# A woven RWKV scan: a later solve, DMA readers tied to program order, and loads issued from ScalarE's queue

## The chip, the cores and the metric

The kernel runs on one core of one Trainium2 chip. The metric is the device time of one execution in microseconds (us). The program is 52362 instructions long, without loops at run time: everything is unrolled when it is built.

## The reference, cut to what matters

Two layers of a diffusion backbone: 1024 latent tokens and 256 context tokens, 1024 channels. Each layer projects the modulated norm of the tokens into four head groups, mixes them, projects the result back with a gated residual, and ends with a SwiGLU FFN. The modulation vectors come from c and w_mod.

```
mod_x = (jax.nn.silu(c) @ w_mod[l] + b_mod[l])[:, None, :]
sh1, sc1, gt1, sh2, sc2, gt2 = jnp.split(mod_x, 6, axis=-1)
ux = _modulate(h, norm1_g[l], sh1, sc1) @ w_in[l]
...
h = h + gt1 * _mix_and_project(ux, y_rwkv_x, *other)
h = h + gt2 * _swiglu(_modulate(h, norm2_g[l], sh2, sc2), ffn_w_in[l], ffn_w_out[l])
```

The part that matters here is the RWKV-7 head group, a recurrence over tokens in both directions, four heads of 64 channels:

```
def step(S, inp):
    w_t, kk_t, a_t, k_t, v_t = inp[:5]
    sa = jnp.einsum('bhvk,bhk->bhv', S, -kk_t)
    S = (S * w_t[:, :, None, :] + sa[..., None] * (kk_t * a_t)[:, :, None, :]
         + v_t[..., None] * k_t[:, :, None, :])
    y = jnp.einsum('bhvk,bhk->bhv', S, inp[5]) if with_out else None
    return S, y
```

## The kernel before

The recurrence is cut into stages of 128 tokens for each direction, two chunks of 64 each: two stages for the context and eight for the latent tokens, ten in a layer. Inside a chunk the steps are replaced by matrix products, for which a triangular matrix has to be inverted for each head, direction and chunk.

A stage goes through these functions, all generators that hand control back at each `yield`:

- `prep` (L870 on) computes the decays and scaled keys of a stage.
- `inner` multiplies them (tiles ps), masks the products on VectorE (L982, four instructions a stage, tiles W), and stores the 32x32 diagonal blocks to a DRAM tile `Ad` (L986, eight DMAs). It loads all blocks back into two tiles `As`, each block row copied to four groups of 32 partitions (L992, two DMAs; in the rows this is `t<-Ad`, since all such tiles are called t). Then comes the solve: first the 4x4 diagonal blocks (L1020 to L1024, one half on VectorE, one on GpSimd after a memset, L1018), then eight block rows (L1032, L1033, L1039 to L1041) on VectorE, all with a raised priority (`s.ahead(SPRI)`). The last reduction, the eighth L1033, ends a solve. The inverse is stored to a DRAM tile `Td` (L1045) and loaded back in another layout into `TT` (L1051, four DMAs).
- `front_b` brings v into place, and merges the two 32x32 inverses into a 64x64 one: a transpose of TT on VectorE (L1091), two groups of small matmuls, and a copy by DMA (L1109).
- `chain` is the recurrence proper: per chunk the products G (copied by ScalarE at L1143), U (L1156), the new state (L1165) and y (L1178), each a group of small matmuls into a pc bank and a copy by ScalarE.
- `finish` adds the two directions, normalizes and gates; it reads what a stage in the other direction has stored.

`rwkv2` weaves them. In iteration `it` the chain of stage it runs beside `front_b` of stage it+1, `inner` of stage it+2 and `prep` of stage it+3, in 14 gaps (GAPS). Each gap advances every live generator by one `yield` (`W.step`), every second gap the chain by one step, and a budget of other matmuls is filled in (`W.fill`, FILL): dense projections, the Fourier mixer, the output projection `outp` and the context's FFN, all into pf banks. At the end of an iteration the generators that the next one needs are run out (`W.drain`). Buffers come from rings (`rg`): As has a depth of 1, Tt of 2, TT and W of 3.

Before that, `rwkv1` makes the projections while the convolution and the pooling run at their side. There the modulation of the first layer is also computed, in six pieces (j, half): by default `mod_sum`, on ScalarE and GpSimd for half 0 and on VectorE for half 1 (L257 and seven times L255 for each of two columns); pieces named in MODPE go to TensorE instead (`mod_pe`).

The order in which instructions stand on an engine is not the order in which they are written. A scheduler places them when the program is built, by priority (the order of writing, less what `ahead` subtracts) and by a model of when each becomes ready. On the chip each engine's queue then runs strictly in that order. All DMAs of this kernel are issued by SyncE (SP), whose queue is in order as well.

## Time and profile before

| | |
|---|---|
| median of 3 runs | 3368.19 us (3366.14 to 3374.23) |
| profiled execution | 3355.82 us, of which 3354.0 us are the span from first to last instruction |
| TensorE (PE) busy | 2962.7 us (88%) |
| VectorE (DVE) busy | 2136.8 us (64%) |
| ScalarE (ACT) busy | 1261.7 us (38%) |
| GpSimd (POOL) busy | 1395.4 us (42%) |
| mean granted TensorE clock | 0.912 of full speed |
| DMA | 415.48 MB, 39.5% of 16 engines, all on one queue |

Busy time is an average over stages with different limits, so it says little by itself. The views by stretch, the chain that ended last and the waits of each engine are read together: a stretch in which no engine is full has something in series, and the waits name it. A wait is printed as who waited, for whom, the total in us, how often, and the longest.

### The profile page before, as it was taken

How to read it: one execution, taken by the hardware profiler on the slowest of the kernel's cores; microseconds unless marked ns; L12 is line 12 of the kernel's file. 1: busy time of each engine (PE TensorE's matmuls, PEld its weight loads, DVE VectorE, ACT ScalarE, POOL GpSimd, SP SyncE). 2: the span in 40 equal slices, each digit the busy share in tenths (PEclk: the TensorE clock that was granted, in tenths of full speed). 3: DMA queues.
4: the chain of work that ended last, by engine and by line, in shares of the span. 5: the costliest groups of instructions: out<-in, count | busy, mean ns of one | idle time of the engine just before them, and what ended most of it. 6: DMA issues, size and time to landing. Idle time of an engine off the chain costs nothing.

```text
span 3354.0 us, 52362 instructions
## 1 busy us (share of the span) xinstructions
PE 2962.7 (88%) x18872; PEld 2391.2 (71%) x18872; DVE 2136.8 (64%) x3524; ACT 1261.7 (38%) x2575; POOL 1395.4 (42%) x1490
## 2 busy tenths in 40 slices
PE   6978898777989999999999978878776699999998
PEld 3757766665778888887888766645554478888887
DVE  6799766666566888644535597666575655555435
ACT  4555435344463322223212455333433433333312
POOL 2465324554268544444310154245541265454600
PEclk8979887788899999999999988878877799999999
DMA  7433345555464444336412222345553322224512
GB/s 265 148 99 105 102 117 143 148 152 156 142 215 153 143 134 151 112 106 225 141 29 90 75 69 95 106 130 142 163 143 83 129 76 82 88 76 134 171 40 77
DMA packets 375818, 415.48 MB, mean 124 GB/s; under 512 B 115587, under 2 KB 214916, under 8 KB 375558
## 3 DMA queue, kind: packets, MB, share of 16 engines
q1 hardware_dynamic: 375558, 412.13, 39.5%
q8 instruction: 149, 2.44, 0.3%
q14 instruction: 111, 0.91, 0.1%
HBM read 306.49 MB, written 100.27 MB: 121 GB/s over the span
## 4 chain that ended last, share of the span: by engine, by line
PE 58%; DVE 21%; DMA 11%; issue 4%; SPq 2%; ACT 2%; POOL 1%; DVEq 0%; POOLq 0%; ACTq 0%
PE pc L151 17%; PE ps L151 17%; PE pb L151 14%; PE pf L151 10%; DVE c L525 4%; DMA t<-Ad 3%; DMA Td<-t 2%; DVE t L1039 2%; DVE t L1032 1%; DVE t L255 1%; DVE t L947 1%; DVE g L1040 1%; DVE t L1041 1%; DVE f L319 1%; DMA Ad<-t 1%
## 5 line engine op out<-in xcount | busy, mean ns | idle before, releaser
L151 PE MATMUL pc<-t,f 128*128 128x512 f32 (+1 forms) x3108 | 744.8, 389 | 31.4 <-ACT t L420 18.7
L151 PEld LDWEIGHTS pc<-t,f 128*128 128x128 f32 x3108 | 575.3, 193 | 160.3 <-ACT t L420 22.9
L151 PE MATMUL ps<-t,f 128*128 128x512 f32 (+1 forms) x2094 | 517.7, 392 | 21.3 <-ACT t L318 7.6
L151 PE MATMUL pb<-t,f 128*128 128x512 f32 (+1 forms) x2094 | 467.5, 368 | 7.8 <-ACT t L1457 3.6
L151 PEld LDWEIGHTS ps<-t,f 128*128 128x128 f32 x2094 | 390.6, 190 | 102.2 <-ACT t L318 8.1
L151 PEld LDWEIGHTS pb<-t,f 128*128 128x128 f32 x2094 | 368.7, 189 | 77.7 <-ACT t L1457 4.4
L1504 ACT CAST f<-c 128x512 fp32r<-128x512 f32 x316 | 195.8, 621 | 529.3 <-PE ps L151 127.7
L1506 POOL TENSOR_TENSOR f<-c,f 128x512 fp32r<-128x512 f32 x135 | 185.8, 1377 | 429.3 <-ACT f L1504 424.2
L151 PE MATMUL pf<-t,f 128*128 128x512 f32 (+2 forms) x1500 | 311.1, 361 | 20.9 <-DMA f<-eo 10.0
L151 PEld LDWEIGHTS pf<-t,f 128*128 128x128 f32 (+1 forms) x1500 | 247.5, 197 | 66.5 <-issue 10.4
L318 ACT CAST f<-m 128x512 fp32r<-128x512 f32 (+1 forms) x236 | 135.5, 577 | 413.4 <-PE pb L151 218.6
L1506 DVE TENSOR_TENSOR f<-c,f 128x512 fp32r<-128x512 f32 x181 | 161.8, 894 | 139.5 <-ACT f L1504 134.5
L523 POOL TENSOR_TENSOR c<-c,cp 128x352 f32<-128x352 f32 (+2 forms) x168 | 185.4, 1104 | 151.5 <-ACT c L516 91.8
L151 PE MATMUL pf<-c,f 128*128 128x512 f32 (+1 forms) x704 | 212.0, 431 | 8.5 <-DVE t L1669 7.2
L319 POOL TENSOR_TENSOR t<-c,t 128x512 fp32r<-128x512 f32 (+1 forms) x110 | 138.1, 1294 | 163.0 <-PE ps L151 100.2
L151 PE MATMUL ps<-t,t 64*128 64x128 f32 (+2 forms) x1032 | 156.1, 342 | 54.9 <-DVE t L947 32.4
L151 PEld LDWEIGHTS ps<-t,t 64*128 64x128 f32 (+1 forms) x1032 | 129.9, 230 | 82.8 <-issue 26.3
L525 DVE SCALAR_TENSOR_TENSOR c<-c,dv,c 128x352 f32<-128x352 f32 (+2 forms) x238 | 186.9, 819 | 1.0
L255 DVE SCALAR_TENSOR_TENSOR cp<-m,sc,cp 128x512 f32<-128x512 f32 x140 | 138.5, 1010 | 51.9 <-DMA m<-in_wmod 51.1
L151 PE MATMUL pc<-t,t 128*64 128x64 f32 (+3 forms) x2484 | 137.8, 246 | 33.8 <-ACT t L1165 19.7
L151 PEld LDWEIGHTS pc<-t,t 128*64 128x64 f32 (+2 forms) x2484 | 111.9, 151 | 76.8 <-issue 24.4
L151 PEld LDWEIGHTS pf<-c,f 128*128 128x128 f32 x704 | 137.4, 222 | 39.8 <-DVE t L1669 7.8
(256 smaller groups left out, 4760.6 us busy)
## 6 DMA issues: line engine op xcount, KB each, us to landing
c<-in_ffin SPq DMA_DIRECT2D x176, 256.0 KB
m<-in_wmod SPq DMA_DIRECT2D x116, 256.0 KB
t<-rw SPq DMA_DIRECT2D x232, 128.0 KB
hid<-t SPq DMA_DIRECT2D x88, 256.0 KB
c<-hid SPq DMA_DIRECT2D x88, 256.0 KB
m<-in_ffout SPq DMA_DIRECT2D x80, 256.0 KB
t<-in_wmod SPq DMA_DIRECT2D x76, 256.0 KB
m<-in_win SPq DMA_DIRECT2D x64, 256.0 KB
```

The lines of the kernel that those rows point to most:

```text
L151: s.nc.tensor.matmul(o, l, r, start=start, stop=stop)
L255: nc.vector.scalar_tensor_tensor(acc[t], w, sc, acc[t], ALU.mult, ALU.add)
L318: s.nc.scalar.copy(hi, src)
L319: (eng or s.lo_eng).tensor_tensor(lo, src, hi.bitcast(F32), ALU.subtract)
L523: nc.gpsimd.tensor_tensor(g, g, t_, ALU.add)
L525: nc.vector.scalar_tensor_tensor(a, w[:, j:j + m], tap(j), a, ALU.mult, ALU.add)
L947: nc.vector.tensor_tensor(BKv[rows, :, :, 1 - h, :], cv(kd)[rows], cv(iP)[rows], ALU.mult)
L1032: nc.vector.tensor_tensor(tv, at(x, o, [0, m], [1, 4], [32, 4]), at(T_, r0, [32, m], [0, 4], [1, 4]), ALU.mult)
L1039: nc.vector.tensor_tensor(tv, at(x, o + 4, [0, m], [1, n], [32, 4]), at(T_, r0, [32, m], [0, n], [1, 4]), ALU.mult)
L1040: nc.vector.tensor_reduce(uv, tv, mybir.AxisListType.X, ALU.add)
L1504: nc.scalar.copy(hi, x)
L1506: (nc.gpsimd if s.nw % 7 in LOP else nc.vector).tensor_tensor(lo, x, hi.bitcast(F32), ALU.subtract)
```

## The change

The readers of data that come by DMA get `pin`: `keep_in_program_order` adds the rule that an instruction may not be placed ahead of what was written before it on its engine. The solve starts three steps later (SLAG), the merge three (MLAG), the read-out two (FLAG), the casts of `outp` four (OLAG). `inner` is run out in the middle of the next iteration rather than at the end of its own. Two more pieces of the modulation go to TensorE. The loads from Ad and from Td are issued by ScalarE, the first after the first half of the copies of T, the second two steps after the store.

```
-MLAG = 3
+MLAG = 6
+SLAG = 3
+FLAG = 4
...
-MODPE = ((3, 0),)
+MODPE = ((2, 1), (3, 0), (4, 1))
...
+    def pin(s, i):
+
+        return s.tc.keep_in_program_order(i)
...
     def split(s, src, hi, lo, eng=None):
-        s.nc.scalar.copy(hi, src)
+        r = s.nc.scalar.copy(hi, src)
         (eng or s.lo_eng).tensor_tensor(lo, src, hi.bitcast(F32), ALU.subtract)
+        return r
...
+                if g == GAPS // 2:
+                    W.drain(tx.get(it + 1))
...
-            for t in (tb_ if 0 <= it + 1 < N else None, tx.get(it + 2), tp if it + 3 < N else None):
+            for t in (tb_ if 0 <= it + 1 < N else None, tp if it + 3 < N else None):
                 W.drain(t)
...
-        for a in range(2):
-            nc.sync.dma_start(As[a], Adf[:, a * 512:(a + 1) * 512].unsqueeze(0).broadcast_to([4, 32, 512]))
...
             yield
+            if not d:
+                for a in range(2):
+                    s.pin(nc.scalar.dma_start(As[a], Adf[:, a * 512:(a + 1) * 512].unsqueeze(0).broadcast_to([4, 32, 512])))
+            yield
+        for _ in range(SLAG):
             yield
         s.lab(f"rsolve.{F.seg}{F.i}")
...
-            nc.gpsimd.memset(at(x, 16 * a, [33, 16]), 1.0)
+            s.pin(nc.gpsimd.memset(at(x, 16 * a, [33, 16]), 1.0))
             with s.ahead(SPRI):
-                e.tensor_tensor(t(0, [1, 2]), D(34, [33, 2]), D(1, [33, 2]), ALU.mult)
+                s.pin(e.tensor_tensor(t(0, [1, 2]), D(34, [33, 2]), D(1, [33, 2]), ALU.mult))
...
         nc.sync.dma_start(Td.rearrange("b u h (m par) i -> par (b u h) m i", par=4), Tt[:, 0:256])
+        for _ in range(2):
+            yield
+        s.lab(f"rsolve.{F.seg}{F.i}")
...
-                nc.sync.dma_start(TTv[r0:r0 + 32, :, 32 * b:32 * b + 32], Td[b, :, h].rearrange("u c i -> c u i"))
+                s.pin(nc.scalar.dma_start(TTv[r0:r0 + 32, :, 32 * b:32 * b + 32], Td[b, :, h].rearrange("u c i -> c u i")))
...
-            nc.scalar.copy(vr[:, p * 128:(p + 1) * 128], s.nat(F.v, p, 1))
+            s.pin(nc.scalar.copy(vr[:, p * 128:(p + 1) * 128], s.nat(F.v, p, 1)))
...
-        nc.vector.transpose(T1.rearrange("q (u i) -> q u i", i=32), TTv[:, :, 0:32])
+        s.pin(nc.vector.transpose(T1.rearrange("q (u i) -> q u i", i=32), TTv[:, :, 0:32]))
...
-        yield
-        yield
+        for _ in range(FLAG):
+            yield
         lab()
         for t_, w_ in ((y, w[0]), (ks, w[1])):
             hv = lambda a: a.rearrange("q (d n) -> q d n", d=2)
-            nc.vector.tensor_tensor(hv(t_), hv(t_), hv(w_)[:, ::-1, :], ALU.add)
+            s.pin(nc.vector.tensor_tensor(hv(t_), hv(t_), hv(w_)[:, ::-1, :], ALU.add))
...
-            s.split(y, *a)
+            late.append((y, a))
             acts.append(a)
+        for _ in range(OLAG):
+            yield None
+        for y, a in late:
+            s.pin(s.split(y, *a))
             yield 0.1
```

What the scheduler makes of it is shown for the last stage of layer 0, its matrices Ad (7682 before, 7554 in the change) and the inverse Td of the stage ahead of it (7649 before, 7660 in the change). Lines of the change are some 6 to 20 higher: L995 is the store to Ad, L1013 the load from it, L1057 the store to Td, L1066 the load from it, L991 the mask, L1032 the first step of a solve, L1045 its reduction, L1106 the transpose of TT, L1158, L1171, L1180 and L1193 the four copies of the chain, L1008 the copy of T.

SP's queue before:

```order
L1045 DMA Td_7649<-t_744_3437 4x256x32
L1337 DMA t_1461_8700<-ho_858 128x256
L1337 DMA t_1462_8701<-ho_859 128x256
L1337 DMA t_1462_8701<-ho_860 128x256
L1051 DMA t_958_4782<-Td_7649 32x8x32 x4
L986 DMA Ad_7682<-t_701_3210 32x4x32 x2
L986 DMA Ad_7682<-t_703_3212 32x4x32 x2
L1670 DMA ho_862<-t_1310_7621 128x512
L296 DMA m_1394_8249<-in_wout 128x512
L992 DMA t_721_3310<-Ad_7682 128x1x512
L992 DMA t_722_3311<-Ad_7682 128x1x512
```

SP's queue in the change:

```order
L995 DMA Ad_7554<-t_700_3187 32x4x32 x2
L995 DMA Ad_7554<-t_702_3189 32x4x32 x2
L876 DMA t_744_3427<-rw_897 128x2x128
L302 DMA m_1385_8205<-in_wout 128x512
L995 DMA Ad_7554<-t_701_3188 32x4x32 x2
L302 DMA m_1388_8211<-in_wout 128x256
L995 DMA Ad_7554<-t_703_3190 32x4x32 x2
L1680 DMA t_1450_8619<-hd_869 128x512
L1680 DMA t_1460_8667<-hd_870 128x512
L1057 DMA Td_7660<-t_751_3480 4x256x32
L302 DMA m_1400_8336<-in_wout 128x512
```

The stores to Ad, half of which stood behind the loads from Td, now stand ahead of the store to Td, and the two loads are gone from this queue.

ScalarE's queue in the change, where these loads went (before, no DMA stands in it):

```order
L1013 DMA t_721_3288<-Ad_7554 128x1x512
L1013 DMA t_722_3289<-Ad_7554 128x1x512
L1180 COPY t_880_4267<-pc_7672 64x2x128
L1180 COPY t_881_4268<-pc_7672 64x2x128
L1008 COPY t_723_3290<-ps_7686 128x256
L1008 COPY t_724_3291<-ps_7686 128x256
L1193 COPY t_957_4754<-pc_7725 128x2x64 x2
L1066 DMA t_983_4911<-Td_7660 32x8x32 x4
L353 ACT_TABLE_LOAD
L353 ACTIVATE t_811_3887<-pb_7753,cv 128x128
L324 CAST f_1374_8130<-m_1373_8128 128x256
L1158 COPY gg_7777<-pc_7768 128x256
```

The chain's copies of the new state (L1180) stand behind the loads from Ad, and its next copy of G (L1158) behind the loads from Td.

VectorE's queue before, from the end of one solve to the first step of the next:

```order
L1032 TENSOR_TENSOR t_744_3437<-t_722_3311,t_744_3437 128x128
L1033 TENSOR_REDUCE t_744_3437<-t_744_3437 128x8x4
L982 TENSOR_TENSOR t_701_3210<-ps_7708,cv 128x512
L982 TENSOR_TENSOR t_703_3212<-ps_7709,cv 128x512
L1669 SCALAR_TENSOR_TENSOR t_1310_7621<-pf_7623,mod_78,t_1310_7621 128x512
L1213 SCALAR_TENSOR_TENSOR t_886_4322<-pb_7772,t_886_4322 128x512
L1091 STREAM_TRANSPOSE t_853_4103<-t_958_4782 128x256
L347 RECIPROCAL t_813_3925<-t_813_3925 128x128
L1020 TENSOR_TENSOR g_7860<-t_721_3310 128x4x2
```

VectorE's queue in the change, from the last mask to the end of the solve ahead of the same one (the first step, L1032, stands three rows further down):

```order
L991 TENSOR_TENSOR t_703_3190<-ps_7607,cv 128x512
L1053 TENSOR_TENSOR t_751_3480<-t_751_3480,g_7325 128x6x8
L1044 TENSOR_TENSOR t_751_3480<-t_722_3289,t_751_3480 128x112
L1045 TENSOR_REDUCE t_751_3480<-t_751_3480 128x7x4
L1228 SCALAR_TENSOR_TENSOR t_884_4279<-pb_7720,t_884_4279 128x512
L1051 TENSOR_TENSOR t_751_3480<-t_722_3289,t_751_3480 128x112
L1052 TENSOR_REDUCE g_7325<-t_751_3480 128x28
L1053 TENSOR_TENSOR t_751_3480<-t_751_3480,g_7325 128x7x4
L1044 TENSOR_TENSOR t_751_3480<-t_722_3289,t_751_3480 128x128
L1045 TENSOR_REDUCE t_751_3480<-t_751_3480 128x8x4
L1688 SCALAR_TENSOR_TENSOR t_1317_7705<-pf_7707,mod_78,t_1317_7705 128x512
L354 RECIPROCAL t_811_3887<-t_811_3887 128x128
```

The last mask stood behind the end of the solve and now stands nine rows ahead of it. The transpose L1091, which stood ahead of the solve, is gone from here. In other stages of the change the masks still stand at the end of the solve.

## Rows read from the trace of the kernel before

**Rows 1.** Windows: stretch, length, busy us (instructions) of PE/PEld/DVE/ACT/POOL, granted clock, DMA share, GB/s.
```profile
504.60:865.00 360.40, 284.99 (x3020) 224.16 (x3019) 235.65 (x519) 156.10 (x409) 186.38 (x297) 0.81 0.54 150
2176.50:2585.00 408.50, 301.79 (x3174) 222.61 (x3174) 251.45 (x572) 155.25 (x413) 180.60 (x307) 0.78 0.48 133
168.00:252.00 84.00, 59.25 (x282) 45.25 (x282) 81.74 (x101) 43.32 (x82) 54.72 (x45) 0.78 0.31 99
252.00:336.00 84.00, 75.11 (x402) 61.30 (x401) 83.65 (x137) 48.22 (x96) 49.56 (x54) 0.92 0.32 104
```

**Rows 2.** The page's chain that ended last, shares by engine and by line.
```profile
PE 58%; DVE 21%; DMA 11%; issue 4%; SPq 2%; ACT 2%; POOL 1%; DVEq 0%; POOLq 0%; ACTq 0%
PE pc L151 17%; PE ps L151 17%; PE pb L151 14%; PE pf L151 10%; DVE c L525 4%; DMA t<-Ad 3%; DMA Td<-t 2%; DVE t L1039 2%; DVE t L1032 1%; DVE t L255 1%; DVE t L947 1%; DVE g L1040 1%; DVE t L1041 1%; DVE f L319 1%; DMA Ad<-t 1%
```

**Rows 3.** VectorE's waits: for whom, us in total, times, longest.
```profile
DVE g L1020 <- DMA t<-Ad: 143.6, 20, 15.1
...
DVE t L1091 <- DMA t<-Td: 68.0, 15, 7.6
```

**Rows 4.** VectorE's timeline at three starts of a solve: start us, us, instruction, [idle before].
```profile
510.86 0.17 DVE L1020 TENSOR_TENSOR g<-t 128x8 f32<-128x8 f32 x1 [9.74 <-DMA t<-Ad]
...
2182.61 0.17 DVE L1020 TENSOR_TENSOR g<-t 128x8 f32<-128x8 f32 x1 [7.18 <-DMA t<-Ad]
...
2545.16 0.17 DVE L1020 TENSOR_TENSOR g<-t 128x8 f32<-128x8 f32 x1 [7.67 <-DMA t<-Ad]
```

**Rows 5.** VectorE's timeline, a last mask of layer 1.
```profile
2173.30 0.42 DVE L982 TENSOR_TENSOR t<-ps,cv 128x256 f32<-128x256 f32 x1 [1.40 <-PE ps L151]
```

**Rows 6.** VectorE's timeline around the last solve's start in layer 0.
```profile
808.97 0.29 DVE L1033 TENSOR_REDUCE t<-t 128x32 f32<-128x128 f32 x1
809.17 1.28 DVE L982 TENSOR_TENSOR t<-ps,cv 128x512 f32<-128x512 f32 x2
...
825.85 0.17 DVE L1020 TENSOR_TENSOR g<-t 128x8 f32<-128x8 f32 x1 [5.48 <-DMA t<-Ad]
```

**Rows 7.** SP's timeline, DMA issues in the same stretch.
```profile
809.28 0.57 SPq L1045 DMA_DIRECT2D Td<-t  x1
...
814.06 1.80 SPq L1051 DMA_DIRECT2D t<-Td  x4
816.22 1.79 SPq L986 DMA_DIRECT2D Ad<-t  x4
...
819.27 1.15 SPq L992 DMA_DIRECT2D t<-Ad  x2
```

**Rows 8.** VectorE's timeline, ends of the first and last solve meant.
```profile
490.21 0.29 DVE L1033 TENSOR_REDUCE t<-t 128x32 f32<-128x128 f32 x1
...
2528.31 0.29 DVE L1033 TENSOR_REDUCE t<-t 128x32 f32<-128x128 f32 x1
```

**Rows 9.** Instructions on Ad: count, shortest, median and longest ns.
```profile
L992 SPq DMA_DIRECT2D t<-Ad x40: 512/558/5698, 383.2 to 2538.9; - x40
```

**Rows 10.** Instructions on Td, the same columns.
```profile
L1051 SPq DMA_DIRECT2D t<-Td x80: 302/443/1296, 430.7 to 2577.5; - x80
```

**Rows 11.** TensorE's waits for two copies of the chain.
```profile
PE pc L151 <- ACT gg L1143: 22.6, 7, 6.0
PE pc L151 <- ACT t L1165: 19.7, 6, 9.0
```

**Rows 12.** ScalarE's waits.
```profile
ACT c L318 <- DMA t<-ymix: 38.8, 11, 7.8
...
ACT t L1001 <- PE ps L999: 36.7, 22, 8.2
```

**Rows 13.** VectorE's groups, 84 to 420 us: xcount, busy us, mean ns, idle before.
```profile
L255 DVE SCALAR_TENSOR_TENSOR t<-t,sc,t 128x512 f32<-128x512 f32 x42 | 40.3, 991 | 0.0
...
L257 DVE TENSOR_SCALAR t<-t,sc 128x512 f32<-128x512 f32 x6 | 6.5, 1119 | 0.0
```

**Rows 14.** TensorE's group of one modulation piece, 84 to 420 us.
```profile
L151 PE MATMUL pf<-t,sc 128*2 128x512 f32 x16 | 9.0, 647 | 3.1 <-DMA t<-in_wmod 3.1
```

More of the change, by code (lines that the diff above doesn't have):

```diff
@@ L1642, in outp @@
         s.lab("outp")
-        acts = []
+        acts, late = [], []
         for k in ks:
```

## The prediction

> **What bounds the kernel now.** Start with the windows by stage [rows 1]. In the two stretches in which the RWKV head group is scanned, 504.6 to 865 us and 2176.5 to 2585 us, no engine is full: TensorE is busy for 285.0 of 360.4 us and 301.8 of 408.5 us, VectorE for 235.7 and 251.5, at a granted clock of 0.81 and 0.78. So something there runs in series. Further up, from 168 to 336 us, VectorE is full (81.7 and 83.7 of 84 us) and TensorE idles for 24.8 + 8.9 = 33.6 us. Next the chain that ended last [rows 2]: matmuls dominate, but 3% of the span (about 100 us) is the load t<-Ad, 2% the store Td<-t, and the lines L1032 and L1039 of the solve stand beside them. The waits say the same [rows 3]: VectorE stood 143.6 us, 20 times, at L1020, the first instruction of a solve, until its load from Ad had landed, and 68.0 us at L1091 until the load from Td had. Twenty is the number of stages, ten in each layer.
>
> Then the rhythm. L1020 starts at 510.86 us and, seven stages later, at 825.85 [rows 4, 6]: 45.0 us a stage. In layer 1 it starts at 2182.61 and, eight stages later, at 2545.16 [rows 4]: 45.3 us. Both layers keep one period although they weave in different other work, so a ring inside the stage sets it. One turn can be read where the last solve of layer 0 begins. The solve before it ends at 809.26 us (808.97 + 0.29) and the masks L982 that make the next matrices end at 810.45 [rows 6]. SP issues the store Td at 809.28, and the next thing it can do for this ring is to wait for that store, because the loads L1051 that read it stand in its queue: they go out from 814.06 to 815.86. Only then do the last four stores L986 to Ad go (816.22 to 818.01), then L992 at 819.27, and L1020 starts at 825.85 [rows 6, 7]. From mask to first step 15.4 us passed, from solve to solve 16.6 us. Where no Td load stood in the way, as in the second solve of layer 1, mask end 2173.72 to L1020 at 2182.61 took 8.9 us [rows 4, 5]. Over the sixteen such gaps inside the two layers (the first from the solve's end at 490.50 to 510.86, the last from 2528.60 to 2545.16 [rows 4, 8]) solve to solve takes 16.1 us in the mean, and mask to first step 12.7 us; so the masks end 3.4 us behind the solve before.
>
> **The change part by part.** *The queue.* L1051 leaves SP's queue, so Ad's last stores no longer stand behind a wait for Td; the change's SP rows show them ahead of Td. Taken alone this is worth 12.7 - 8.9 = 3.8 us a gap.
>
> *The order.* In the change's VectorE rows the masks of a stage stand at least five rows ahead of the end of the solve before in 7 of these 16 gaps, and close to it or behind it in 9. In the 9 I leave the masks 3.4 us behind the solve, as now: the gap is 3.4 + 8.9 = 12.3 us. In the 7 the 8.9 us lie beside the rest of the solve; I leave 3 us, between 0 and 8.9. The mean gap becomes (7 x 3 + 9 x 12.3) / 16 = 8.2 us, 7.9 less than now; this contains the queue's 3.8.
>
> *What ScalarE pays.* A stage gives it six more issues. On SP they took 0.558 us (Ad) and 0.443 us (Td) at the median [rows 9, 10], so 2 x 0.558 + 4 x 0.443 = 2.9 us. No DMA is issued from ScalarE in this trace, so SP's durations are the nearest rows; the lower bound is 0. It also takes over the wait for Td, 4.8 us in the turn above (809.28 to 814.06 [rows 7]), of which the two added yields may hide all. Behind these instructions stand the copies of the recurrence, L1158 and L1180 of the change, and TensorE waits for such copies already (22.6 us for L1143, 19.7 us for L1165 [rows 11]). Together 0 to 7.7 us; ScalarE has idle time, but not at a fixed place, and I take half, 3.85 us.
>
> So a gap gains 7.9 - 3.85 = 4.05 us, and 16 gaps 65 us. Is there room? TensorE is busy for 285.0 / 8 = 35.6 us a stage in layer 0 [rows 1], so a period of 45.2 - 4.05 = 41.1 us still fits, VectorE's 29.5 us too; a gain of 7.9 us would leave TensorE 1.7 us of slack.
>
> *Modulation.* Two of the pieces that VectorE sums go to TensorE: 28 steps L255 of 0.991 us and 4 starts L257 of 1.119 us [rows 13], 32.2 us off the engine that is full there. One such piece cost TensorE 9.0 us in that stretch [rows 14], so two cost 18 us of its 33.6 idle; 15.6 us are left and cap the gain. I take 15 us, between 0 and 32.
>
> *At no cost.* The later merge (MLAG 6) and read-out (FLAG 4) lie in woven steps with other matmuls ahead of them; without that cover each would add one wait at L1106, at most the 7.6 us that L1091 now waits [rows 3]. The casts of outp come after four steps: the 38.8 us that ScalarE waited at L318 for t<-ymix [rows 12] go. In exchange the woven projection pauses four more steps in each of five calls; those matmuls run later, in stages that have TensorE idle. I count both as zero.
>
> **Sum:** 65 + 15 = 80 us. The profiled execution took 3355.82 us around a span of 3354.0; it becomes 3276. It was 12.4 us under the median of the three runs, 3368.19, so the forecast for a median is 3288 us.
>
> **The rivals.** *The hand-over is hidden almost whole.* ScalarE loses nothing: 16 x 7.9 = 126 us, with the 15 us: 3227 us. For it: ScalarE is busy for 19.5 us of a stage's 45 [rows 1]. Against: TensorE would have to run almost without waits. Chance 0.20.
>
> *Only issue time is saved.* The two loads from Ad end about 6 us after they are issued (819.27 to 825.85 [rows 6, 7]), and if the order still puts each solve just behind its load, all that SP is spared is 2.9 us of issues a stage: 16 x 2.9 = 46 us, with the 15 us: 3307 us. The 8.9 us of an unblocked stage [rows 4, 5] speak against a gain in the transfer itself, the 15.4 us of a blocked one [rows 6] for more than issue time. The Trainium skill, "DMA: Bandwidth & Descriptors", section "Issuing engines are not separate DMA queues", says that DMAs started from ScalarE or SP run on the same 16 DMA engines and that several starting engines save only the sequencer's issue time; by that rule this rival is the result, and the change's last part would be worth little more than its issues. The trace agrees on the transfer, but shows a wait at the head of SP's queue that a second queue does avoid. Chance 0.20.
>
> *The ring closes elsewhere.* VectorE waits as long as now, for masks or for the load, and only the modulation pays: 3353 us. For it: nine gaps keep mask and first step together. Chance 0.15.
>
> *ScalarE becomes the place of the wait, and the kernel is slower.* The loads of Ad stand behind copies that wait for TensorE (up to 8.2 us at L1001 [rows 12]), and in front of the copies that feed TensorE; TensorE then comes late to the next stage's masks, and the ring runs through ScalarE. It decides the sign once ScalarE adds more than 7.9 us a stage, plus the 15 us spread over 16 gaps, 0.9: 8.8 us. With 10 us, of the 7.7 us above and part of such a wait, the loop loses 2.1 x 16 = 34 us, less the 15: 3387 us. Against: ScalarE's waits already end at TensorE, so part of it would be waited anyway. Chance 0.13.
>
> **How the numbers follow.** The forecast has 0.32. A difference under 0.3%, about 10 us, can't be told from no change here. Faster by more: forecast 0.32, hidden whole 0.20, issue time 0.20, and of the rival at 3353 (15 us under the median) half, 0.08: 0.80. The rest of that rival is no change, 0.07. Slower 0.13. The range runs from 3215, which takes in most of the hidden case, to 3375, which takes in the rival at 3353 and leaves out most of the slower one; about 0.08 lies outside at either end.
>
> **What would show it.** Right: VectorE's wait at its first solve step (now L1032) falls below 100 us; the starts of that step are 40 to 42 us apart; ScalarE shows waits for Ad and Td of some 30 to 80 us together; SP's stores to Ad follow their masks within 2 us; from 168 us on VectorE sums 32 tiles fewer. The order step is wrong if the wait at L1032 stays at 143 us while the masks stand ahead of the solve's end. The ScalarE step is wrong if TensorE's waits for copies do not grow, or if they take back the whole gain. A period of 45 us with a shorter start would mean that the ring closes elsewhere; a time over 3378 us, that ScalarE holds it.

## The result and the profile after

The change is slower: 3403.23 us (median of 4 runs, 3399.70 to 3409.82) against 3367.16 us (median of 4), a ratio of 1.0121 with a 95% interval of 1.0101 to 1.0142. The forecast was 3288 us; the rival in which ScalarE becomes the place of the wait said 3387 us. The profiled execution took 3405.68 us, its span is 3403.9 us, 49.9 us more than the span before.

Where the 50 us lie can be read from the starts of the first step of a solve (L1020 before, L1032 now) and the ends of its last reduction, taken from VectorE's timelines of the traces; the last three columns are runs told of below:

| stretch, us | before | change | modulation alone | casts as before | spread on before |
|---|---|---|---|---|---|
| to the first solve | 389.8 | 391.2 | 389.6 | 393.1 | 386.6 |
| first solve to end of the last, layer 0 | 461.6 | 463.8 | 453.3 | 483.1 | 414.8 |
| from there to the first solve of layer 1 | 1264.1 | 1293.7 | 1273.3 | 1265.9 | 1265.0 |
| first solve to end of the last, layer 1 | 454.0 | 459.9 | 446.3 | 451.6 | 410.8 |
| from there to the end | 784.5 | 795.3 | 781.0 | 791.8 | 780.8 |

The scans are longer instead of shorter, and the two stretches behind them lose more still: 29.6 and 10.8 us. The windows of the change, cut at the same loads as those of before [rows 1] (the third of layer 0, the second of layer 1), with the stretch behind the scan of layer 0 as fifth row:

```profile
496.75:865.00 368.25, 283.43 (x2988) 222.90 (x2989) 226.97 (x512) 146.15 (x393) 177.83 (x290) 0.76 0.50 137
2207.18:2620.00 412.82, 310.71 (x3028) 235.00 (x3028) 247.52 (x563) 149.12 (x400) 176.71 (x306) 0.74 0.45 128
168.00:252.00 84.00, 70.06 (x302) 49.19 (x301) 65.03 (x85) 42.14 (x79) 53.41 (x45) 0.82 0.26 84
252.00:336.00 84.00, 75.03 (x429) 61.76 (x427) 83.11 (x133) 54.63 (x110) 54.40 (x61) 0.98 0.30 98
865.00:1071.00 206.00, 174.93 (x1369) 146.26 (x1368) 118.98 (x149) 101.05 (x197) 102.65 (x75) 0.93 0.50 161
```

TensorE's granted clock in the two scans fell from 0.81 and 0.78 to 0.76 and 0.74. From 168 to 252 us VectorE is relieved (65.0 us busy where it was 81.7), as the modulation's step said; from 252 to 336 us it is as full as before (83.1 and 83.7 us). The chain that ended last shows less of t<-Ad and more of ScalarE than before [rows 2]:

```profile
PE 61%; DVE 19%; DMA 10%; issue 4%; ACT 3%; POOL 2%; SPq 1%; ACTq 0%; DVEq 0%; POOLq 0%
PE pc L153 18%; PE ps L153 17%; PE pb L153 15%; PE pf L153 10%; DVE c L532 4%; DMA t<-Ad 2%; DMA Td<-t 2%; DMA t<-Td 2%; DVE t L1051 1%; DVE t L1044 1%; DVE t L956 1%; DVE t L947 1%; DVE g L1052 1%; DVE t L1053 1%; DVE t L1497 1%
```

VectorE's waits changed as they were meant to [rows 3]: 109.1 us at the first step instead of 143.6, and 20.1 us at the transpose instead of 68.0. But what it no longer waits for there, it waits for elsewhere; the third row was 33.0 us before (at L347).

```profile
DVE g L1032 <- DMA t<-Ad: 109.1, 15, 12.8
...
DVE t L354 <- ACT t L353: 61.7, 14, 12.8
...
DVE t L1106 <- DMA t<-Td: 20.1, 7, 5.5
```

In five of the 16 gaps between solves the first step has no idle time before it at all, so there the load was not the last thing that the solve waited for. The starts in both layers, to be read as those of before [rows 4]:

```profile
503.03 0.17 DVE L1032 TENSOR_TENSOR g<-t 128x8 f32<-128x8 f32 x1 [10.16 <-DMA t<-Ad]
...
2213.22 0.17 DVE L1032 TENSOR_TENSOR g<-t 128x8 f32<-128x8 f32 x1 [7.26 <-DMA t<-Ad]
...
833.50 0.17 DVE L1032 TENSOR_TENSOR g<-t 128x8 f32<-128x8 f32 x1
...
2593.18 0.17 DVE L1032 TENSOR_TENSOR g<-t 128x8 f32<-128x8 f32 x1
```

From 503.03 to 833.50 us are seven stages of 47.2 us (45.0 before), from 2213.22 to 2593.18 eight of 47.5 us (45.3 before). It is not the gaps between solves that grew: from the end of one to the start of the next 15.3 us pass in the mean, 16.1 before. The solves themselves, from the first step to the last reduction, take 31.8 us instead of 29.4 (mean of the sixteen ahead of these gaps). VectorE works on their instructions as long as before (15.6 and 15.3 us of each), but stands idle for 4.0 us inside a solve instead of 1.6. The last two of the four rows have no idle time in front of them, although their first loads had been issued 11 and 21 us earlier: VectorE's queue held other work ahead of them. SP's rows show what the prediction expected of it, for the stage of its example [rows 7]:

```profile
816.17 0.78 SPq L995 DMA_DIRECT2D Ad<-t  x2
817.00 0.90 SPq L1680 DMA_DIRECT2D t<-hd  x2
820.97 0.60 SPq L1057 DMA_DIRECT2D Td<-t  x1
```

The stores to Ad go out at 816.17 us, right behind the last mask (it ends at 816.14 us) and ahead of the store to Td. In the mean of the 16 gaps the last store goes out 2.2 us behind the last mask, 4.3 before. ScalarE's rows show the price, one stage from 635 to 656 us:

```profile
635.66 0.53 ACTq L1013 DMA_DIRECT2D t<-Ad  x1
...
643.03 0.51 ACTq L1013 DMA_DIRECT2D t<-Ad  x1
643.58 0.43 ACT L1193 COPY t<-pc 128x128 f32<-128x128 f32 x2 [4.61 <-DVE t L1044]
...
652.39 2.12 ACTq L1066 DMA_DIRECT2D t<-Td  x4
654.55 0.74 ACT L1171 COPY t<-pc 64x256 f32<-64x256 f32 x2 [8.88 <-DMA t<-Td]
```

The second load from Ad is issued 7.4 us after the first, because it writes a buffer that the solve before has still to read; one other stage shows such a wait (2.9 us), and in the other 18 the second goes out about 0.5 to 1.1 us after the first. The four loads from Td stand at the head of the queue until the store (issued at 644.54 us) has landed, and the recurrence's copy L1171 stands behind them: ScalarE's compute side is idle for 8.88 us before it, and it starts 3.3 us after the last of its matmuls (651.2 us). Summed from the end of ScalarE's row before to the issue, ScalarE stood 20.6 us in front of the loads from Ad and 59.1 us in front of those from Td, and it spent 63.5 us on issuing them: 143 us, 7.2 us for each of the 20 stages. (Expectations below speak of 94 us of standing, and of 46 us for the short transfers; counted this way it is 79.7 and 35.9 us.) The counts and durations of these issues (shortest, median, longest ns), which answer to those on SP [rows 9, 10]:

```profile
L1013 ACTq DMA_DIRECT2D t<-Ad x40: 514/531/1103, 385.4 to 2572.6; - x40
...
L1066 ACTq DMA_DIRECT2D t<-Td x80: 309/462/3148, 455.9 to 2614.7; - x80
```

### The profile page after: what moved, and what is told of

Same layout as the page of the kernel before. It is cut to its first block, busy times and chain, and to the rows that moved or that the text cites. A ratio compares the mean times of both kernels' runs of the same rounds, so it can differ in the third digit from the quotient of the medians.

```text
span 3403.9 us, 52415 instructions
## 1 busy us (share of the span) xinstructions
PE 3005.7 (88%) x18888; PEld 2419.2 (71%) x18888; DVE 2107.5 (62%) x3498; ACT 1256.5 (37%) x2575; POOL 1383.8 (41%) x1484
## 4 chain that ended last, share of the span: by engine, by line
PE 61%; DVE 19%; DMA 10%; issue 4%; ACT 3%; POOL 2%; SPq 1%; ACTq 0%; DVEq 0%; POOLq 0%
PE pc L153 18%; PE ps L153 17%; PE pb L153 15%; PE pf L153 10%; DVE c L532 4%; DMA t<-Ad 2%; DMA Td<-t 2%; DMA t<-Td 2%; DVE t L1051 1%; DVE t L1044 1%; DVE t L956 1%; DVE t L947 1%; DVE g L1052 1%; DVE t L1053 1%; DVE t L1497 1%
## 5 line engine op out<-in xcount | busy, mean ns | idle before, releaser
L153 PE MATMUL pf<-c,f 128*128 128x512 f32 (+1 forms) x704 | 197.8, 420 | 19.7 <-POOL c L325 9.0
L153 PE MATMUL ps<-t,t 64*128 64x128 f32 (+2 forms) x1032 | 167.3, 348 | 42.4 <-DVE t L991 13.0
L153 PE MATMUL pc<-t,t 128*64 128x64 f32 (+3 forms) x2484 | 153.6, 262 | 39.6 <-ACT t L1171 15.8
L153 PEld LDWEIGHTS ps<-t,t 64*128 64x128 f32 (+1 forms) x1032 | 140.3, 237 | 66.9 <-issue 18.7
L153 PEld LDWEIGHTS pc<-t,t 128*64 128x64 f32 (+2 forms) x2484 | 124.8, 165 | 87.8 <-issue 33.4
```

The lines of the kernel that those rows point to most:

```text
L153: s.nc.tensor.matmul(o, l, r, start=start, stop=stop)
```

## The experiments

All ratios are to the kernel before on the same chip, with 95% intervals. The medians that it had beside these runs lie between 3356.93 and 3367.16 us, so kernels are compared by their ratios. In short:

| kernel | median us | ratio |
|---|---|---|
| the change | 3403.23 | 1.0121 (1.0101 to 1.0142) |
| change, loads on SyncE | 3361.42 | 0.9997 (0.9983 to 1.0011) |
| change, casts as before | 3382.76 | 1.0070 (1.0051 to 1.0088) |
| change, lags as before | 3371.31 | 1.0038 (1.0020 to 1.0056) |
| before, modulation alone | 3343.84 | 0.9952 (0.9935 to 0.9970) |
| before, queue alone | 3388.01 | 1.0075 (1.0051 to 1.0099) |
| change, Td loads on SyncE | 3379.59 | 1.0054 (1.0030 to 1.0078) |
| before, spread | 3260.06 | 0.9703 (0.9681 to 0.9724) |
| before, spread and modulation | 3276.84 | 0.9749 (0.9727 to 0.9771) |
| change, solve untied | 3382.40 | 1.0070 (1.0049 to 1.0090) |
| change, two buffers As | 3403.06 | 1.0115 (1.0083 to 1.0146) |
| change, Td loads later | 3392.95 | 1.0084 (1.0055 to 1.0112) |
| change, spread | 3296.28 | 0.9799 (0.9759 to 0.9839) |
| before, queue and modulation | 3386.63 | 1.0075 (1.0057 to 1.0093) |
| ties and places alone, with modulation | 3360.22 | 1.0006 (0.9992 to 1.0020) |
| change, spread, loads on SyncE | 3286.42 | 0.9786 (0.9768 to 0.9804) |
| before, store to Td in four | 3344.31 | 0.9957 (0.9942 to 0.9972) |

**The queue undone.**

```
-                    s.pin(nc.scalar.dma_start(As[a], ...
+                    s.pin(nc.sync.dma_start(As[a], ...
-                s.pin(nc.scalar.dma_start(TTv[r0:r0 + 32, ...
+                s.pin(nc.sync.dma_start(TTv[r0:r0 + 32, ...
```

> The change with the loads of Ad and of Td issued by SyncE again, at the places in the program and with the ties that the change gives them; ScalarE issues no DMA. Theory A (ScalarE became the place of the wait: its 94 us of waits in front of Ad and Td loads, 4.7 us a stage, delay the recurrence's copies): the time falls back by at least 16 x 2.2 = 35 us to 3368 us or less, and the stage period returns from 47.3 to about 45 us. Theory B (the later merge, read-out and casts push the output projection's matmuls out of the scan, and the stage period is set by the new order): the time stays at 3385 to 3420 us and 50 or more matmuls of outp still stand behind the first layer's scan.

The ratio falls from 1.0121 to 0.9997, which is 1.24%, some 42 us: theory A's number, and the largest single part. What is left is no different from the kernel before. The period is 44.7 and 45.3 us, as theory A asks. The price shows where TensorE waits for ScalarE: in the two scans (from the first solve's start to the last one's end in each layer) this was 54.5 us before, is 83.2 us in the change and 31.6 us here. The masks' stores go out as early as in the change, 2.3 us behind the last mask in the mean, so the places in the program were enough for that. (The profiled execution took 3376.97 us, 16 us more than the median, so its stretches are a little long.)

**The casts undone.** The delay and the tie ahead of the casts in `outp` go, all else stays:

```
-            late.append((y, a))
+            s.split(y, *a)
             acts.append(a)
+            yield 0.1
-        for _ in range(OLAG):
-            yield None
-        for y, a in late:
-            s.pin(s.split(y, *a))
-            yield 0.1
```

> The change with the casts of the output projection as they were (each right behind its load's issue, no tie, no four steps of delay before them); all else as in the change. Theory B: the output projection starts about 20 us earlier in the scan, the 54 matmuls more that ran behind the first layer's scan go back into it, and of the 22 us lost between 840 and 1040 us about 15 to 22 come back: 3380 to 3388 us. Theory A: nothing comes back, 3395 to 3410 us.

0.5% or 17 us come back, but not just as theory B put it. The stretch behind layer 0's scan falls by 27.8 us, to what it was before, and the scan itself grows by 19.3 us (table above). The group of the output projection's matmuls behind that scan, first in the kernel before (865 to 1040 us), then in the change (865 to 1071 us):

```profile
L151 PE MATMUL pf<-c,f 128*128 128x512 f32 x54 | 15.7, 412 | 0.0
```

```profile
L153 PE MATMUL pf<-c,f 128*128 128x512 f32 x110 | 30.8, 405 | 0.0
```

So 56 more matmuls, 15 us of TensorE, stand behind 865 us with casts that came four steps later. Counted from the end of the last solve it is 128 of them in the change, 79 before and 55 here. Late casts do lighten the scan, and the work comes back at its end: in all nine kernels here with the late casts 128 stand there, and the last of them ends 58 to 62 us behind the last solve, against 29 to 44 us in the other nine.

**The lags undone.**

```
-MLAG = 6
-SLAG = 3
-FLAG = 4
+MLAG = 3
+SLAG = 0
+FLAG = 2
```

> The change with MLAG 3, SLAG 0 and FLAG 2 as before; queue, ties and casts as in the change. Theory C (the lags lengthen the stage: solve, merge and read-out come late for the chain of the next iteration): the period falls to 45 us or less and the end of each layer's scan comes 10 us sooner, 3365 to 3380 us. Theory A: no change within 10 us, 3393 to 3413 us.

0.83% or 28 us come back, and the period is 45.2 and 44.6 us, about that of before, as theory C asks. The 42, 17 and 28 us of these three are not to be added: each was measured with the other parts in place, and together they exceed the loss.

**The modulation alone.**

```
-MODPE = ((3, 0),)
+MODPE = ((2, 1), (3, 0), (4, 1))
```

> The kernel before with only the two modulation pieces moved to TensorE. The prediction's step says 15 us gained: 3352 us. The drift between the two traces up to 420 us says that only 3 to 5 us come of it: 3362 us. If the lower granted clock or the order downstream eats it: 3367 us or more.

16 us faster, the size of the prediction's term. But the table above shows that none of it had been gained when the first solve starts (389.6 against 389.8 us): it arises in the two scans, in layer 1 too, where no piece of the modulation was moved. In the change VectorE's groups from 84 to 420 us lost the 28 steps, but TensorE's pieces now wait 9.0 us for their weights where the one piece waited 3.1 [rows 13, 14]:

```profile
L261 DVE SCALAR_TENSOR_TENSOR t<-t,sc,t 128x512 f32<-128x512 f32 x14 | 12.6, 940 | 0.2 <-DMA t<-in_wmod 0.2
...
L263 DVE TENSOR_SCALAR t<-t,sc 128x512 f32<-128x512 f32 x2 | 2.7, 1410 | 0.1
```

```profile
L153 PE MATMUL pf<-t,sc 128*2 128x512 f32 x48 | 27.7, 669 | 9.0 <-DMA t<-in_wmod 9.0
```

The number was right and the place was not; why the scans gained is open.

**The queue alone.** Kernel before, the two `nc.sync.dma_start` of the loads from Ad and Td written `nc.scalar.dma_start`, nothing else.

> The kernel before with both loads issued from ScalarE's queue and nothing else changed: no lags, no ties, no later casts, the TT loads right behind the store of Td. Theory A (ScalarE's queue is the wrong place, whatever else is changed: it stands still 4.8 us for each store of Td and its copies feed TensorE): slower by 35 us or more, 3390 us or above, with 80 to 100 us of waits for Td on ScalarE. Theory D (the queue costs only together with the lags and ties, which put the loads in front of copies that are due): within 10 us of before. The prediction's step on the queue (3.8 us a gap gained, ScalarE's share 3.85 lost): no change either.

It is slower by 0.75%, 25 us, between the two theories. ScalarE stood 127.6 us in front of the loads from Td here, 6.4 us a stage, since they follow right behind the store, and TensorE's waits for ScalarE in the two scans rose from 54.5 to 79.8 us. The queue costs without lags or ties too. What it gives is small: from mask to first step 11.3 us pass in the mean instead of 12.7.

**Only the loads from Td back.**

```
-                s.pin(nc.scalar.dma_start(TTv[r0:r0 + 32, ...
+                s.pin(nc.sync.dma_start(TTv[r0:r0 + 32, ...
```

> The change with only the four loads from Td back on SyncE; the two loads from Ad stay on ScalarE. If the wait for the store of Td on ScalarE is what costs (94 us of waits, 73 of them for Td): most of the 42 us that both loads together gave back in the first experiment, 3365 to 3372 us. If the loads from Ad cost it: at most 12 us back, 3390 us or more.

1.0121 becomes 1.0054: of the 1.24% the loads from Td carry 0.67 and those from Ad the other 0.57. Neither forecast held; it is not the wait for Td alone.

**The transfer itself made shorter.** The kernel before, with the partitions of the solve numbered so that the four copies of a row lie side by side. The tables of constants follow; the store to Td becomes four.

```
-            nc.sync.dma_start(As[a], Adf[...].unsqueeze(0).broadcast_to([4, 32, 512]))
+            nc.sync.dma_start(As[a], Adf[...].unsqueeze(1).broadcast_to([32, 4, 512]))
...
-        nc.sync.dma_start(Td.rearrange("b u h (m par) i -> par (b u h) m i", par=4), Tt[:, 0:256])
+        Tdv = Td.rearrange("b u h (m par) i -> par (b u h) m i", par=4)
+        for par in range(4):
+            nc.sync.dma_start(Tdv[par], Tt[par::4, 0:256])
...
-            tinit[32 * par:32 * par + 32, m_, 4 * m_ + par] = 1
+            tinit[par::4, m_, 4 * m_ + par] = 1
```

> The kernel before with the partitions of the solve numbered otherwise (four copies of a row side by side instead of 32 apart), so that the source of the loads from Ad has 32 as its outermost size instead of 4; the store to Td becomes four stores by remainder. Queues and order of writing stay. If the loads run on 4 of the 16 DMA engines now, each should land some 2.5 us sooner and the second of the pair about 5 us; if the ring through the solve sets the stage, 20 stages gain 2.5 to 5 us each less 1.7 us for the three added issues: 16 to 66 us, 3290 to 3340 us. If the ring closes elsewhere: the wait at the first step falls from 143 us to 100 us or less, and the time does not change by more than 10 us.

It is 3.0% faster, about 100 us, more than the 16 to 66 us expected, with 60 more DMAs on SP, the masks still behind the solve in 12 of 16 gaps (13 before) and the loads from Td still in SP's way. It beats both kernels. SP's and VectorE's rows at the last stage of layer 0, and VectorE's wait for Ad in that trace (143.6 us before):

```profile
774.24 0.92 SPq L986 DMA_DIRECT2D Ad<-t  x2
...
776.41 1.22 SPq L992 DMA_DIRECT2D t<-Ad  x2
```

```profile
499.69 0.17 DVE L1020 TENSOR_TENSOR g<-t 128x8 f32<-128x8 f32 x1 [8.85 <-DMA t<-Ad]
...
779.56 0.17 DVE L1020 TENSOR_TENSOR g<-t 128x8 f32<-128x8 f32 x1 [3.28 <-DMA t<-Ad]
```

```profile
DVE g L1020 <- DMA t<-Ad: 68.0, 17, 8.8
```

From issue to first step it takes 3.2 us (776.41 to 779.56), against 6.6 us [rows 6, 7]; over the 16 gaps this part falls from 5.8 to 3.0 us on average counted from the end of the first issue, and the gap between solves from 16.1 to 11.2 us. The period of layer 0, 45.0 us before [rows 4, 6], is 40.0 us here (499.69 to 779.56 us, seven stages). The Trainium skill, "DMA: Bandwidth & Descriptors", section "Why a DMA increments its semaphore by 16 and not by 1", says that a DMA uses the largest number of engines up to 16 that divides the outermost sizes on both sides (sizes of 1 left out); an estimate from this rule is 4 for the loads as they were (4 and 128) and 16 for these (32 and 128). The traces agree with it: the semaphore that tells of a load's landing is raised five times for each of the 40 loads before, as a rule once about 1 us after the issue and four times at the landing, and sixteen times for each load here. From issue to the last raise a load takes 7.2 us before and 3.5 us here at the median, and the store to Td (five raises before, sixteen for each of the four here) 4.8 us and about 2 us.

**Spread and modulation.** Both edits on the kernel before.

> As the one before, with the two modulation pieces on TensorE too. If the parts add up: 16 us less than the spread alone. If the order of the whole shifts: not more than 5 us from it, either way.

It takes 3276.84 us, which by the ratios is 15 us slower than the spread alone, where the modulation had gained 16 us without it. Neither expectation held. The modulation's gain depends on the order of the rest.

**The solve untied.**

```
-            s.pin(nc.gpsimd.memset(at(x, 16 * a, [33, 16]), 1.0))
+            nc.gpsimd.memset(at(x, 16 * a, [33, 16]), 1.0)
             with s.ahead(SPRI):
-                s.pin(e.tensor_tensor(t(0, [1, 2]), D(34, [33, 2]), D(1, [33, 2]), ALU.mult))
+                e.tensor_tensor(t(0, [1, 2]), D(34, [33, 2]), D(1, [33, 2]), ALU.mult)
```

> The change without the tie on the first step of the solve (on either engine) and on the memset ahead of it; the other ties, the lags and the queue stay. In the change's trace that first step starts in 5 of 16 stages without any idle time before it, 2 to 15 us after its load must have landed, because other work of VectorE was placed ahead of it: 38 us together. Theory E (the tie undoes the raised priority of the solve, and that is why the gap between solves stayed at 15.3 us): the mean gap falls to 13 us or less and the time by 20 to 40 us, to 3365 to 3385 us. Theory A alone: the step starts sooner, but ScalarE's standing still (7.9 us a stage) sets the stage; no change within 10 us of 3403.

1.0121 becomes 1.0070: 0.5%, some 17 us, and the starts without idle time in front of them go from 5 of 16 to none. The time lies where theory E put it, with a gain a little under its 20 us. Its gap does not: the mean stays at 15.4 us. From the issue of the first load to the first step the time falls back from 8.5 to 5.8 us, as before the change, but the masks now stand ahead of the solve's end in 4 gaps instead of 8. The 17 us lie almost whole in layer 1's scan (442.6 us, 459.9 in the change), so that the tie delays the first step is shown, and what this costs in time is not settled. What the tie does is best seen in the change's last stage, on GpSimd and on VectorE:

```profile
2577.73 0.13 POOL L1030 MEMSET t<- 128x16 f32 x1 [13.26 <-DMA t<-Ad]
2580.67 0.13 POOL L1030 MEMSET t<- 128x16 f32 x1 [2.81 <-DMA t<-Ad]
```

```profile
2574.54 0.68 DVE L1228 SCALAR_TENSOR_TENSOR t<-pb,t 128x512 f32<-128x512 f32 x1
2588.00 0.95 DVE L354 RECIPROCAL t<-t 128x128 f32<-128x128 f32 x1 [12.78 <-ACT t L353]
2592.57 0.69 DVE L1235 TENSOR_TENSOR t<-t,pb 128x512 f32<-128x512 f32 x1 [3.62 <-PE pb L153]
```

GpSimd's memsets on the two matrices follow their landing, at 2577.73 and 2580.67 us. VectorE's first step stands behind L354 and L1235 in the queue, waits through the 12.78 us in which L354 waits for ScalarE, and starts at 2593.18 us, 15 us late. The raised priority of the solve did not lift a tied step over these.

**Two buffers for As.** `s.rg(R, f"As{a}", 1)` becomes `s.rg(R, f"As{a}", 2)`.

> The change with two buffers instead of one for each of the two matrices As, so that the loads of a stage no longer wait until the solve before has read its own. If that wait (35 us in 20 stages on ScalarE, at the second load above all) is a good part of what ScalarE costs, or holds the masks that were moved ahead: 10 to 35 us faster than the change, 3370 to 3393 us. If not: no change within 10 us.

The ratio is 1.0115, no change. The second load now goes out 0.5 to 1.1 us after the first in every stage, so the wait for the solve before is gone, and it had cost nothing that shows.

**The loads from Td later.** `for _ in range(2)` ahead of them becomes `range(4)`.

> The change with four steps instead of two between the store of Td and the loads from it, on ScalarE as before. In the change ScalarE stood 59.6 us in front of these loads and spent 41.9 us on issuing them. If the standing still is what costs: it falls below 20 us, and 15 to 22 us of the time come back, 3381 to 3388 us. If the issues and the place of the loads cost, or if the merge now comes late for lack of TT: no gain, 3395 us or more.

The ratio is 1.0084: 12 us come back, less than the first forecast and more than the second. ScalarE still stood 46.7 us in front of them (59.1 in the change), more than expected: two more written steps shortened the standing by only 12.4 us.

**The spread on the change.** The edits of the spread on the changed kernel.

> The change with the partitions of the solve numbered so that the loads from Ad and the store to Td spread over more DMA engines (as the spread on the kernel before, which gave 3.0%). If the ring through load and solve still sets the stage in the change: a gain of 80 to 100 us, 3300 to 3325 us, and a wait for Td on ScalarE that is shorter by 2 us a stage. If the change moved the bound elsewhere (ties, ScalarE): less than half of it, 3355 us or more.

The ratio is 0.9799, a gain of 3.2% or 107 us, a little more than expected: the transfer's price is as high in the change as before it. ScalarE's standing falls to 16.2 us for Ad and 19.7 us for Td.

**Queue and modulation on the kernel before.** The edits of the fourth and fifth experiments together.

> The kernel before with the two modulation pieces on TensorE and both loads issued from ScalarE; order, lags, ties and casts as before. If the cost of the queue is one of its own (25 us on the kernel before, 42 us on the change): 3344 + 25 to 42 us, 3369 to 3386 us. If it costs only with the later order: 3350 us or less.

The ratio is 1.0075 against 0.9952: the queue costs 1.23%, 41 us, as much as in the change. Its price does not come from the later order. It does depend on the rest: without the modulation it was 25 us, and read the other way, the modulation gains nothing once the loads are on ScalarE (1.0075 with and without it).

**Ties and places alone.** The change with the edits of the first three experiments together. Left of it are the modulation, the ties, the place of the loads in the program, and `inner` run out half an iteration later.

> The change with the loads on SyncE, MLAG 3, SLAG 0, FLAG 2 and the casts as before: what is left is the modulation, the ties, the end of inner in the middle of the next iteration, and the later places of the loads in the program. If the lags and the late casts make the 17 us that the later order cost without the queue: as the modulation alone, 3340 to 3350 us. If the ties and the places of the loads make it: 3357 us or more. The prediction's step on the order asks for 3260 us or less in any of these.

The ratio is 1.0006 against 0.9952 for the modulation alone: 0.54%, 18 us slower. With loads on SyncE, lags and late casts add nothing to this (0.9997). So the later order's cost on SyncE sits in what is left: the ties, the places and the earlier end of `inner`. These were not taken apart. In this trace the first load from Ad is issued 10.4 us after the last mask on average (7.1 with the modulation alone), and VectorE's wait is longer than the 144.9 us there:

```profile
DVE g L1032 <- DMA t<-Ad: 171.3, 19, 15.4
```

**The spread change with the loads on SyncE.** The edits of the first experiment on the change with the spread.

> The change with the spread loads and stores (3296 us) and the loads issued by SyncE. If ScalarE's standing still is what the queue costs, it is now about half (46 us of waits in 20 stages instead of 94) and comes back: 3260 to 3280 us, no better than the spread with modulation alone (3277 us). If the queue's price was tied to the long transfers: within 8 us of 3296 us. If the later order pays once the ring is short: under 3255 us.

The ratio is 0.9786 against 0.9799: once the transfers are short, ScalarE's queue costs nothing that these intervals tell.

**Only the store to Td in four.** The kernel before, each store from `Tt[32 * par:32 * par + 32, 0:256]`, the partitions and the loads from Ad as they were.

> The kernel before with only the store to Td cut into four, one for each group of 32 partitions; the loads from Ad as they were. If the loads from Ad are what the spread shortened: at most 20 us faster than before, 3345 us or more. If the store to Td (landing 4.8 us after its issue) was as much: 3320 us or less.

The ratio is 0.9957, 14 us faster, although the store lands as early as in the spread (2 us after its issue, 4.8 before). If the two parts add, most of the spread's 100 us come from the loads from Ad; these were not made shorter by themselves.

## Why the prediction was wrong

The kernels above can be set in a row in which each holds the one before it. The modulation alone takes 0.9952 of the time before; with the ties, the places and the earlier end of `inner` it is 1.0006, with the lags and late casts too 0.9997, and with the loads on ScalarE, which is the change, 1.0121. In us these steps are -16, +18, -3 (no difference, given the intervals) and +42. The prediction had -15 for the first, and -65 for all the others together.

**What bounds the kernel: right.** A ring through load, solve and masks sets the scan's period. Made shorter at its transfers it gives 5 us a stage and 100 us in all. I took the load's 6 us for fixed and looked for the gain in the order around it; the 8.9 us of an unblocked stage, of which two thirds are this load, pointed at it.

**"The order", 7.9 us a gap with the queue's 3.8 inside: this is the step that failed.** The prediction gave the order and SP's part together 126 us. Measured with the loads on SyncE, the change against the modulation alone is 0.9997 against 0.9952: 15 us lost, where the order without the queue's part (4.1 us a gap) would have gained 66. The queue's part by itself gave 1.4 us from mask to first step, not 3.8. In the change the masks did end ahead of the solve in 8 of 16 gaps (forecast 7), but those gaps took 9.8 us in the mean and not 3, and the others 20.9 and not 12.3; the mean is 15.3 us for a forecast of 8.2 and a start of 16.1. The 3 us were no row: in the kernel before three gaps had their masks ahead already, and they took 8.6 us in the mean. Besides, the sum took the solve's own length for fixed without a reason, and it grew by 2.4 us, more than the gap gave. For the gap two reasons are shown. First, putting masks ahead only helps if the rest of the hand-over follows: from mask to issue of the first load the time fell by 1.3 us (7.0 to 5.7), and from issue to first step it rose by 2.7 us (5.8 to 8.5). Second, the tie on the first step holds it behind unrelated work on VectorE; untied, these 2.7 us are gone, and 17 us of the time come back, though the mean gap stays. I had counted positions in VectorE's queue up to the solve's end and did not look at what stood between there and the tied first step. Why the masks of the other eight stages came later than before, and why VectorE stands longer inside a solve, is not settled.

**"What ScalarE pays", 3.85 of 0 to 7.7 us a stage: too small at the engine, too large in time.** The issues cost it 3.2 us a stage (2.9 forecast). In front of the loads from Td it stood 3.0 us a stage; 4.8 us were forecast with nothing hidden, and 6.4 us were measured without the two steps, so the steps hid about half. In front of the loads from Ad, which the sum left out, it stood 1.0 us. Together these are 7.2 us, near the top of the range. In time it is 42 us, less than the term of 62. The sign that the prediction gave for this step was that TensorE's waits for copies grow. For the two copies of [rows 11] they did not grow together (L1143 and L1165 are L1158 and L1180 now):

```profile
PE pc L153 <- ACT gg L1158: 25.4, 9, 6.9
...
PE pc L153 <- ACT t L1180: 10.6, 4, 7.6
```

Two rows were too narrow a sign: TensorE's waits for all of ScalarE's work in the two scans did grow, from 54.5 to 83.2 us, and fell to 31.6 us without the queue. The waits of ScalarE for Ad and Td, forecast at 30 to 80 us, are 79.7 us. With short transfers the price vanishes (0.9786 against 0.9799), which fits a wait whose length is the transfer's.

**"Modulation", 15 us:** 16 measured alone, but in the scans and not in the stretch that was argued. On the spread kernel it costs 15 us. That the number agreed was luck, and no proof of the step.

**"At no cost": half right.** On SyncE lags and casts together add nothing (0.9997 with them, 1.0006 without); on ScalarE's queue each costs. The casts' matmuls did not find room "in stages that have TensorE idle": some 50 of them ran behind the scan.

**The rivals.** ScalarE as the place of the wait was the one rival on the slow side, and its mechanism is shown in the main: without the queue the change is no slower than before, and TensorE no longer waits so long for ScalarE. That its 3387 us came near is luck in part. They were worked out with the order's gain in the ring, and the order gave none. The rule of the Trainium skill that another issuing engine saves only issue time ("DMA: Bandwidth & Descriptors", section "Issuing engines are not separate DMA queues") gave 3307 us; the measured 42 us of loss do not contradict what it says of the transfer, but show a price on the engine that issues.

## What to carry to other kernels

A load issued from an engine that also computes puts that engine's next work behind the wait for what the load reads; move it there only if that has already landed, or shorten the transfer first. When a transfer is in the ring, look at the outermost size of both its sides before re-ordering anything: here one renumbering of partitions was worth 3%, and the re-ordering around it nothing. A tie to program order protects an instruction from being too early, but it also takes away its priority; read what stands in front of it, not only what it is tied for.

## What the runs showed of the hardware that was not expected

More of the same matmuls ran at the lower clock. The group pc<-t,t of 2484 small matmuls was busy for 137.8 us (mean 246 ns) in the kernel before; in the change, whose scans have a granted clock of 0.76 and 0.74:

```profile
L153 PE MATMUL pc<-t,t 128*64 128x64 f32 (+3 forms) x2484 | 153.6, 262 | 39.6 <-ACT t L1171 15.8
```

The granted clock has two levels in these traces, 1.0 and 0.5 of full speed (2.4 and 1.2 GHz), and 0.76 is a mean of the two. In both traces such a matmul takes 222 ns at the higher level and 314 ns at the lower one (medians, with ends as the profile models them). In the kernel before 386 of the 2484 started at the lower level, in the change 809; the lower level lasted 594 us before and 646 us in the change. TensorE's busy time rose by 43 us (2962.7 to 3005.7) of which the two modulation pieces make 18.7 us at most (27.7 less the 9.0 of one piece [rows 14]). With the queue alone it rose to 2997.0 us with not one matmul more. TensorE did not stand idle longer for that: 391.3 us before, 398.2 in the change, 390.2 with the queue alone. Why the lower level lasted longer is open.

A short DMA landed late when it was issued close behind a long one. In the kernel before a load from Td landed 1.9 us after its issue at the median, in the change 7.4 us. In 12 of the 20 stages of the change the first load from Td goes out within about 3 us behind a load from Ad, and it lands 7.0 to 10.5 us after its issue; in the other eight it takes 1.7 to 4.3 us. With the lags as before the median is 2.5 us, with the loads on SyncE 7.2 us, so it goes with the place in the order and not with the queue. What this cost in time is not shown.
